# A second LayerNorm whose mean is taken out ahead: centred rows of w_down and a centred residual in a decoder layer on one Trainium2 core

## The chip, the cores and the metric

The kernel runs on one core of one Trainium2 chip. The metric is the device time of an execution in microseconds (us). Three executions of the kernel before took 368.48, 368.86 and 370.68 us; the median is 368.86. Profiles are of one execution each. Engines are named as in the profile: PE (TensorE), PEld (its weight loads), DVE (VectorE), ACT (ScalarE), POOL (GpSimd) and SP (SyncE, which issues the loads). L987 is line 987 of the kernel before.

## The reference

One layer over 256 positions of width 1024, all in float32: a mixer of attention and a short convolution, a LayerNorm, a gated feed-forward with a causal convolution of three taps, and a second LayerNorm. The part that matters here:

```python
x = layer_norm(DEEPNORM_ALPHA * x + mix, ln1_g[l], ln1_b[l])
u = causal_dwconv(x @ w_up[l], conv_w_ffn[l])
f = (jax.nn.silu(u[..., :D_FF]) * u[..., D_FF:]) @ w_down[l]
x = layer_norm(DEEPNORM_ALPHA * x + f, ln2_g[l], ln2_b[l])

def layer_norm(x, g, b):
    mu = jnp.mean(xf, axis=-1, keepdims=True)
    var = jnp.mean(jnp.square(xf - mu), axis=-1, keepdims=True)
    y = (xf - mu) * lax.rsqrt(var + LN_EPS) * g + b
```

`w_up` is 1024 by 5632, `w_down` 2816 by 1024. The mean over a row of `f` is `silu(..) * u` times the means over the rows of `w_down`; so if each row of `w_down` has its mean taken out, `f` has mean zero, and the same holds for `x` in the sum.

## The kernel before

Every product is made of three: each float32 operand is split into a high part (rounded by ACT) and a low part (the rest, made by DVE), and high by high, high by low and low by high are summed in PSUM. The weights come packed in chunks of 2048 columns (1 MB), each with two units of 1024; SP loads a chunk into one of three raw buffers (`issue_dma`, L175). `split_h` (L192) makes a unit's high part on ACT, `split_l` (L197) its low part on DVE; nine buffers each hold them until PE has used them. The next load into a raw buffer waits for the splits of both units that lay there.

The order of the feed-forward part is written out by hand. `seq` lists the units as PE uses them: for each pair i of w_up tiles a "g" and a "v" unit, and from i = 3 to 16 a unit d = i - 3 of w_down ("d"); the last eight units of w_down (TAIL) follow as "t". After PE's work of entry k, `slot(k, stages)` puts on ACT the first halves of the stages that are due, then splits so many units that they are four or five entries ahead of PE, and then the stages' DVE halves:

```python
for st, i in stages:
    FFN[st][0](i)
la = LA if k < 20 else LA + 1
while done["h"] < min(len(seq), k + la + 2):
    split_h(seq[done["h"]][2])
```

The four stages of a pair are: copy and sum of its PSUM banks (L807 on ACT, L811 on DVE), three taps of the convolution (L817; L823 and L825), SiLU and product (L830; L834), and the split of the result into an f tile (L837; L841). ACT and DVE run all this in the order in which it is issued. A pair's PSUM banks are two deep.

At the end, `finish(0)` runs the last eight units of w_down for the first 128 rows, one `slot` after each, and `finish(1)` for the other 128 rows: the left 512 columns first, then two pieces of 256 columns in banks of their own (`e`), so that DVE can work on one piece while PE makes the next. `residual` (L742, L744) adds `ALPHA * x1` to a bank and takes the statistics of the piece; `norm_stats` (L720, L721) joins the statistics on DVE and takes the power -1/2 on POOL; `norm_first` (L732) subtracts the mean and multiplies by ln2's factors, `norm_second` (L729) multiplies by the power and adds ln2's offsets; each piece is then stored, the last two from the queues of SP and ACT.

Of the kernel before, what the change touches and what calls it, by code (L numbers as in the profile page):

```python
# [8 lines left out]
F32 = mybir.dt.float32  # L9
# [3 lines left out]
AF = mybir.ActivationFunctionType  # L13
ALU = mybir.AluOpType

P = 128
S = 256
D = 1024
# [6 lines left out]
NP = DFF // P  # L25
ALPHA = 2.0 ** 0.25
EPS = 1e-5
# [110 lines left out]
def layer_kernel(ctx: ExitStack, tc: tile.TileContext, x, wpack, cpack, ln1_g, ln1_b, ln2_g, ln2_b, out):  # L138
    nc = tc.nc
# [4 lines left out]
    tmp = ctx.enter_context(tc.tile_pool(name="tmp", bufs=1))  # L144
# [5 lines left out]
    def acc_bank(name):  # L150
        return psum.tile([P, 512], F32, tag="acc", name=name)

    def ps_bank(name):
        return ps_pool.tile([P, 512], F32, tag="ps", name=name)

    def scratch(shape, name, bufs=None, tag="scr"):
        return tmp.tile(shape, F32, tag=tag, name=name, bufs=bufs or 6)
# [5 lines left out]
    chunks, plan_units, U = plan()  # L163
    blocks = transfers(chunks, plan_units)
    units = [dict(chunk=c, off=off, shape=(k, n), h=None, l=None) for c, off, k, n, _ in plan_units]
    raws = []
    XR_CHUNK = 20

    def issue_dma(c):
        while len(raws) <= c and len(raws) < len(chunks):  # L170
            i = len(raws)
            t = wp.tile([P, CHUNK], F32, tag="raw", name=f"raw{i}", bufs=RAW_BUFS)
            raws.append(t)
            for a, b, off in blocks[i]:
                nc.sync.dma_start(t[:, a:b], wpack[off:off + P * (b - a)].rearrange("(p n) -> p n", p=P))  # L175
            if i == XR_CHUNK:
                nc.sync.dma_start(xr, x[0].rearrange("(t p) d -> p t d", p=P))

    def alloc(u, part, tag):
        k, n = units[u]["shape"]  # L180
        units[u][part] = wp.tile([P, k, n], F32R, tag=tag, name=f"{tag}{u}", bufs=HL_BUFS)
# [6 lines left out]
    def split_h(u):  # L188

        issue_dma(units[u]["chunk"] + RAW_BUFS - 1)  # L190
        alloc(u, "h", "wh")
        nc.scalar.activation(units[u]["h"], raw_of(u), AF.Copy)  # L192

    def split_l(u):

        alloc(u, "l", "wl")
        nc.vector.tensor_tensor(units[u]["l"], raw_of(u), units[u]["h"].bitcast(F32), op=ALU.subtract)  # L197

    def raw_of(u):
        un = units[u]  # L200
        k, n = un["shape"]
        return raws[un["chunk"]][:, un["off"]:un["off"] + k * n].rearrange("p (k n) -> p k n", k=k)
# [43 lines left out]
    neghalf = cst.tile([P, 1], F32, name="neghalf")  # L246
# [25 lines left out]
    cs = cst.tile([P, 2, 2, 8], F32, name="cs")  # L272
# [55 lines left out]
    def cols_wide(u, bank, b):  # L328


        un = units[u]
        for k in range(un["h"].shape[1]):
            nc.tensor.matmul(bank, un["h"][:, k, :], b[:, k].rearrange("p a s -> p (a s)"), start=k == 0, stop=False)  # L333

    def cols_narrow(u, bank, b):

        un = units[u]
        nk = un["l"].shape[1]
        for k in range(nk):
            nc.tensor.matmul(bank[:, 0:S], un["l"][:, k, :], b[:, k, 0], start=False, stop=k == nk - 1)  # L340
# [138 lines left out]
    def slot(u, products=None):  # L479


        if products:
            products()
        mine = beside.pop(u, {})
        for f, a in mine.get("pe", []) + mine.get("act", []):
            f(*a)
        while done["h"] <= u + LA + 1:
            if units[done["h"]]["h"] is None:
                split_h(done["h"])
            done["h"] += 1  # L490
        while done["l"] <= u + LA:
            if units[done["l"]]["l"] is None:
                split_l(done["l"])
            done["l"] += 1
        for f, a in mine.get("dve", []):
            f(*a)
# [160 lines left out]
    for j in range(16):  # L657
        u = U[("g", 0)] + j
# [42 lines left out]
    for half in range(2):  # L701
        for e in range(2):
            ua, uc = U[("ao", half)] + e, U[("co", half)] + e
            for n in range(2):
# [4 lines left out]
                bank = ps_bank(f"y{i}")  # L709
# [7 lines left out]
    def norm_stats(r, stats, pieces):  # L717

        mv = tmp.tile([P, 4], F32, tag="mv", name="mv", bufs=4)
        nc.vector.bn_aggr(mv[:, 0:2], stats[:, 0:pieces, :])  # L720
        nc.gpsimd.tensor_tensor(mv[:, 3:4], mv[:, 1:2], neghalf, op=ALU.pow)  # L721
        return mv

    def norm_apply(o, r, mv, g, b):
        nc.vector.scalar_tensor_tensor(o, r, mv[:, 0:1], g, op0=ALU.subtract, op1=ALU.mult)
        nc.vector.scalar_tensor_tensor(o, o, mv[:, 3:4], b, op0=ALU.mult, op1=ALU.add)

    def norm_second(r, mv, ln, cs):
        nc.vector.scalar_tensor_tensor(r[:, cs], r[:, cs], mv[:, 3:4], ln[:, 1, cs], op0=ALU.mult, op1=ALU.add)  # L729

    def norm_first(r, mv, ln, cs):
        nc.vector.scalar_tensor_tensor(r[:, cs], r[:, cs], mv[:, 0:1], ln[:, 0, cs], op0=ALU.subtract, op1=ALU.mult)  # L732

    x1 = big.tile([P, 2, D], F32, tag="rows", name="x1")
    x1T = big.tile([P, KT, 2, S], F32R, tag="xT", name="x1T")

    def with_eps(stats):

        nc.vector.tensor_scalar(stats[:, 0, 2:3], stats[:, 0, 2:3], EPS * D, None, op0=ALU.add)

    def residual(t, nh, bank, res, r, stats, piece, c0, c1):
        nc.vector.scalar_tensor_tensor(r[:, c0:c1], res[:, t, c0:c1], ALPHA, bank[:, c0 - nh * 512:c1 - nh * 512],  # L742
                                       op0=ALU.mult, op1=ALU.add)
        nc.vector.bn_stats(stats[:, piece, :], r[:, c0:c1])  # L744
        if piece == 0:
            with_eps(stats)
# [44 lines left out]
    ln2 = big.tile([P, 2, D], F32, tag="e8", name="ln2")  # L791
# [87 lines left out]
    def ps_pair(name):  # L879
        return pairs.tile([P, 2, 512], F32, tag="pair", name=name)  # L880
# [7 lines left out]
    dacc = [[acc_bank(f"d{t}{nh}") for nh in range(2)] for t in range(2)]  # L888
# [19 lines left out]
    def take(n):  # L908
# [4 lines left out]
                pending.remove((stage, i))  # L913
        return out


    seq = []
    for c in range(1, NP // 2):
        for e in range(2):
# [3 lines left out]
            d = i - 3  # L923
# [21 lines left out]
    for k, (kind, i, u) in enumerate(seq[:tail_from]):  # L945
        if kind == "g":
            pair, first_unit = ps_pair(f"pb{i}"), u
            cols_wide(u, pair[:, 0], x1T)
        elif kind == "v":
            cols_wide(u, pair[:, 1], x1T)  # L950
            cols_narrow(first_unit, pair[:, 0], x1T)
            cols_narrow(u, pair[:, 1], x1T)
            PB[i] = pair
        else:
            down(i)
        if k == 0:
            up0_T(0)
            up0_T(1)
            pending.extend([(st, p) for p in range(2) for st in (1, 2, 3)])
        stages = take(2 if k > 11 or len(pending) > 6 else 1)  # L960
        if kind == "v":
            stages.insert(0, (0, i))
            pending.extend([(st, i) for st in (1, 2, 3)])
        slot(k, stages)


    def finish(t):
        r = x1[:, t]
        stats = tmp.tile([P, 4, 6], F32, tag="stats", name=f"rstats{t}", bufs=2)
        if t == 0:  # L970
            for k in range(TAIL):
                down(NP - TAIL + k, (t,))
                slot(tail_from + k, take(2))
            assert not pending
            for nh in range(2):
                residual(t, nh, dacc[t][nh], x1, r, stats, nh, nh * 512, nh * 512 + 512)
        else:
            for i in range(NP - TAIL, NP):
                down(i, (t,), (0,))
            nc.vector.scalar_tensor_tensor(r[:, 512:1024], x1[:, t, 512:1024], ALPHA, dacc[t][1], op0=ALU.mult, op1=ALU.add)  # L980
            for c in range(2):
                residual(t, 0, dacc[t][0], x1, r, stats, c, c * 256, c * 256 + 256)
            for c in range(2, 4):
                bank = ps_pair(f"e{c}")[:, 0]
                for i in range(NP - TAIL, NP):
                    down_part(i, bank, c)
                nc.vector.tensor_tensor(r[:, c * 256:c * 256 + 256], r[:, c * 256:c * 256 + 256], bank[:, 0:256], op=ALU.add)  # L987
                nc.vector.bn_stats(stats[:, c, :], r[:, c * 256:c * 256 + 256])
        mv = norm_stats(r, stats, 2 if t == 0 else 4)
        if t == 0:  # L990
            for c in range(2):
                cc = slice(c * 512, (c + 1) * 512)
                norm_apply(r[:, cc], r[:, cc], mv, ln2[:, 0, cc], ln2[:, 1, cc])
                nc.sync.dma_start(out[0, t * P:(t + 1) * P, cc], r[:, cc])
            return
        for c in range(2):
            norm_first(r, mv, ln2, slice(c * 512, c * 512 + 512))
        for cc, queue in ((slice(0, 640), nc.sync), (slice(640, D), nc.scalar)):
            norm_second(r, mv, ln2, cc)
            queue.dma_start(out[0, t * P:(t + 1) * P, cc], r[:, cc])  # L1000

    for t in range(2):
        finish(t)
# [42 lines left out]
```

## Time and profile before

| | |
|---|---|
| median of three runs | 368.86 us (368.48 to 370.68) |
| profiled execution | 369.0 us, span 367.1 us |
| granted TensorE clock, mean | 0.997 |
| PE busy | 358.0 us, 98% of the span |
| DVE busy | 294.9 us, 80% |
| ACT busy | 217.0 us, 59% |
| POOL busy | 7.0 us, 2% |
| read from HBM | 68.24 MB |

Times in the profile count from the first instruction; the span ends with the last. A row of the timeline has the start and the duration in us, the engine, the line, the operation, the tiles written and read, and the shapes; in square brackets stands how long the engine was idle ahead of it and what ended that. A row of a group has the count after x, then the busy time in us and the mean of one in ns. The next instruction of ACT or DVE can start before the last one's end, by about 0.1 us. A row of stretches has for each engine the busy time and the count of instructions, then the granted clock, the share of the DMA engines and GB/s.

### The profile page before, as it was taken

What the parts mean: (1) busy time and instruction counts of PE and PEld (TensorE: products, weight loads), DVE (VectorE), ACT (ScalarE), POOL (GpSimd) and SP (SyncE); (2) the same over time, 40 slices, a digit from 0 to 9 for tenths busy, and PEclk for the clock granted to TensorE, in tenths of its full rate; (3) what the DMA queues carried; (4) which work ended last, traced back from release to release, by engine and by line L of the source; (5) the groups of instructions that cost most, each with busy time, mean ns of one, the idle gap of its engine ahead of it and who ended that gap; (6) DMA issues with size and microseconds to landing.
All of it is one profiled execution on the core that took longest, in us unless ns stands there. A gap on an engine that the chain in (4) does not pass through costs nothing.

```text
span 367.1 us, 5335 instructions
## 1 busy us (share of the span) xinstructions
PE 358.0 (98%) x2022; PEld 312.2 (85%) x2022; DVE 294.9 (80%) x510; ACT 217.0 (59%) x372; POOL 7.0 (2%) x26
## 2 busy tenths in 40 slices
PE   8999999999999999999999999999999999999991
PEld 7888888888888899988888888888888888888891
DVE  4696887788895679869769988987869696999784
ACT  4685776747867654634266666575657566676300
POOL 2000000000000000102000000000000000000000
PEclk9999999999999999999999999999999999999998
DMA  7978565333853634596360835448182645662011
GB/s 263 356 292 318 180 225 211 114 114 129 331 214 130 221 124 137 190 357 224 124 223 12 341 121 221 153 193 309 46 334 90 254 140 204 228 237 108 0 59 57
DMA packets 11241, 69.63 MB, mean 190 GB/s; under 512 B 1232, under 2 KB 1616, under 8 KB 4176
## 3 DMA queue, kind: packets, MB, share of 16 engines
q1 hardware_dynamic: 10496, 67.00, 50.0%
q0 software_dynamic: 576, 2.10, 1.8%
q8 instruction: 16, 0.26, 0.3%
q10 hardware_dynamic: 144, 0.20, 0.1%
q14 instruction: 9, 0.07, 0.1%
HBM read 68.24 MB, written 1.05 MB: 189 GB/s over the span
## 4 chain that ended last, share of the span: by engine, by line
PE 97%; DVE 1%; DMA 1%; DVEq 0%; SPq 0%; issue 0%
PE pb L333 20%; PE pb L340 10%; PE g L333 8%; PE d L305 5%; PE d L306 5%; PE d L307 5%; PE g L340 4%; PE q L555 3%; PE k L555 3%; PE v L555 3%; PE b L333 2%; PE y L326 2%; PE y L325 2%; PE y L324 2%; PE c L333 2%; PE o L307 2%
## 5 line engine op out<-in xcount | busy, mean ns | idle before, releaser
L197 DVE TENSOR_TENSOR wl<-raw,wh 128x1024 fp32r<-128x1024 f32 x90 | 109.8, 1221 | 23.3 <-ACT wh L192 22.7
L192 ACT ACTIVATE wh<-raw 128x1024 fp32r<-128x1024 f32 x90 | 94.5, 1055 | 22.7 <-DMA raw<-in_wpack 22.6
L333 PE MATMUL pb<-x1T,wh 128*128 128x512 f32 x320 | 76.2, 390 | 0.0
L333 PEld LDWEIGHTS pb<-x1T,wh 128*128 128x128 f32 x320 | 59.7, 188 | 12.1
L220 DVE TENSOR_TENSOR wl<-raw,wh 128x1024 fp32r<-128x1024 f32 (+1 forms) x38 | 38.0, 1037 | 7.4 <-ACT wh L219 7.1
L340 PEld LDWEIGHTS pb<-x1T,wl 128*128 128x128 f32 x320 | 41.0, 191 | 1.6
L340 PE MATMUL pb<-x1T,wl 128*128 128x256 f32 x320 | 41.5, 283 | 0.0
L219 ACT ACTIVATE wh<-raw 128x1024 fp32r<-128x1024 f32 (+1 forms) x38 | 32.9, 904 | 14.3 <-DMA raw<-in_wpack 8.5
L333 PE MATMUL g<-xT,wh 128*128 128x512 f32 x128 | 31.4, 393 | 0.0
L305 PE MATMUL d<-wh,f 128*128 128x512 f32 x80 | 31.3, 391 | 0.0
L306 PE MATMUL d<-wl,f 128*128 128x512 f32 x80 | 31.3, 391 | 0.0
L307 PE MATMUL d<-wh,f 128*128 128x512 f32 x80 | 31.1, 389 | 0.0
L333 PEld LDWEIGHTS g<-xT,wh 128*128 128x128 f32 x128 | 23.3, 188 | 4.5
L807 ACT ACTIVATE fb<-pb 128x512 f32<-128x512 f32 x20 | 11.9, 595 | 23.8 <-PE pb L340 23.8
L825 DVE SCALAR_TENSOR_TENSOR fc<-fb,consts,fc 128x254 f32<-128x254 f32 x40 | 19.3, 484 | 1.4
L823 DVE SCALAR_TENSOR_TENSOR fc<-fb,consts,fc 128x255 f32<-128x255 f32 x40 | 19.1, 478 | 0.0
L817 ACT ACTIVATE fc<-fb,consts 128x256 f32<-128x256 f32 x40 | 17.9, 496 | 0.4 <-DVE fb L811 0.4
L307 PEld LDWEIGHTS d<-wh,f 128*128 128x128 f32 x80 | 15.0, 188 | 3.2
L305 PEld LDWEIGHTS d<-wh,f 128*128 128x128 f32 x80 | 15.1, 189 | 2.7
L306 PEld LDWEIGHTS d<-wl,f 128*128 128x128 f32 x80 | 15.1, 189 | 2.6
L340 PEld LDWEIGHTS g<-xT,wl 128*128 128x128 f32 x128 | 16.4, 191 | 0.6
L340 PE MATMUL g<-xT,wl 128*128 128x256 f32 x128 | 16.6, 283 | 0.0
(183 smaller groups left out, 606.1 us busy)
## 6 DMA issues: line engine op xcount, KB each, us to landing
raw<-in_wpack SPq DMA_DIRECT2D x55, 1024.0 KB, 4.9
raw<-in_wpack SPq DMA_DIRECT2D x6, 896.0 KB, 5.5
xr<-in_x SPq DMA_DIRECT2D x1, 1024.0 KB, 7.6
ln<-in_ln_g POOLq DMA_DIRECT2D x2, 512.0 KB, 5.6
ln<-in_ln_b POOLq DMA_DIRECT2D x2, 512.0 KB, 6.2
raw<-in_wpack SPq DMA_DIRECT2D x3, 256.0 KB, 3.4
raw<-in_wpack SPq DMA_DIRECT2D x1, 512.0 KB, 5.8
out<-x SPq DMA_DIRECT2D x2, 256.0 KB, 2.1
```

Source lines behind the costliest of these rows:

```text
L192: nc.scalar.activation(units[u]["h"], raw_of(u), AF.Copy)
L197: nc.vector.tensor_tensor(units[u]["l"], raw_of(u), units[u]["h"].bitcast(F32), op=ALU.subtract)
L219: nc.scalar.activation(h, src, AF.Copy)
L220: (eng or nc.vector).tensor_tensor(l, src, h.bitcast(F32), op=ALU.subtract)
L305: nc.tensor.matmul(o, ah, bh, start=start, stop=False)
L306: nc.tensor.matmul(o, ah, bl, start=False, stop=False)
L307: nc.tensor.matmul(o, al, bh, start=False, stop=stop)
L333: nc.tensor.matmul(bank, un["h"][:, k, :], b[:, k].rearrange("p a s -> p (a s)"), start=k == 0, stop=False)
L340: nc.tensor.matmul(bank[:, 0:S], un["l"][:, k, :], b[:, k, 0], start=False, stop=k == nk - 1)
L555: nc.tensor.matmul(banks[m][t], (xl if p == 2 else xh)[:, k, t * P:(t + 1) * P], wl if p == 1 else wh, start=k == 0 and p == 0, stop=k == ...
L823: nc.vector.scalar_tensor_tensor(c[:, 1:S], pb[:, a * S:a * S + S - 1], w_ffn(1, j), c[:, 1:S], op0=ALU.mult, op1=ALU.add)
L825: nc.vector.scalar_tensor_tensor(c[:, 2:S], pb[:, a * S:a * S + S - 2], w_ffn(0, j), c[:, 2:S], op0=ALU.mult, op1=ALU.add)
```

## The change

The units of w_down (`CENTRED`) are split so that each row has its mean taken out: ACT makes a first pass that writes the unit times -1/1024 and sums it (the sum is minus the mean, `m`), and a second pass that adds `m` as a bias and rounds; DVE's low part becomes (raw + m) - high. For each half of 128 rows, `centred(t)` makes `x1 = ALPHA * x1` in place on ACT with its sum, and minus the mean of it in a tile of one column; these are put on ACT's queue behind entries 14 and 17 of `seq`. In `finish` the residual is added with that mean (`add_residual`), the sum of squares over 1024, starting at LN_EPS, runs from piece to piece in `var` (`squares`), ln2's factors are multiplied piece by piece as soon as the squares of a piece are taken (`times_factors`), and POOL takes the power -1/2 of the last sum. `store` is the former `norm_second` with the store. PE's instructions and the loads are the same as before, in the same order.

```diff
+    CENTRED = {U[("dn", d)] + e for d in range(NP // 2) for e in range(2)}
...
         alloc(u, "h", "wh")
-        nc.scalar.activation(units[u]["h"], raw_of(u), AF.Copy)
+        h, raw = units[u]["h"], raw_of(u)
+        if u in CENTRED:
+            m = units[u]["m"] = tmp.tile([P, 1], F32, tag="wm", name=f"wm{u}", bufs=8)
+            nc.scalar.activation(h, raw, AF.Copy, scale=-1.0 / D, accum_out=m)
+            nc.scalar.activation(h, raw, AF.Identity, bias=m)
+        else:
+            nc.scalar.activation(h, raw, AF.Copy)
...
-        nc.vector.tensor_tensor(units[u]["l"], raw_of(u), units[u]["h"].bitcast(F32), op=ALU.subtract)
+        if u in CENTRED:
+            nc.vector.scalar_tensor_tensor(units[u]["l"], raw_of(u), units[u]["m"], units[u]["h"].bitcast(F32),
+                                           op0=ALU.add, op1=ALU.subtract)
...
+    def centred(t):
+        m = tmp.tile([P, 2], F32, tag="xm", name=f"xm{t}", bufs=2)
+        nc.scalar.activation(x1[:, t], x1[:, t], AF.Copy, scale=ALPHA, accum_out=m[:, 0:1])
+        nc.scalar.activation(m[:, 1:2], m[:, 0:1], AF.Copy, scale=-1.0 / D)
+        XM[t] = m[:, 1:2]
...
         slot(k, stages)
+        if k in (14, 17):
+            centred((k - 14) // 3)
...
+    def add_residual(t, cc, bank):
+        nc.vector.scalar_tensor_tensor(x1[:, t, cc], bank, XM[t], x1[:, t, cc], op0=ALU.add, op1=ALU.add)
+
+    def squares(t, cc, var, c):
+        r = x1[:, t, cc]
+        n = cc.stop - cc.start
+        nc.vector.tensor_tensor_reduce(out=scratch([P, n], f"sq{t}{c}"), in0=r, in1=r, scale=1.0 / D,
+                                       scalar=var[:, c - 1:c] if c else EPS, op0=ALU.mult, op1=ALU.add,
+                                       accum_out=var[:, c:c + 1])
+
+    def times_factors(t, cc):
+        nc.vector.tensor_tensor(x1[:, t, cc], x1[:, t, cc], ln2[:, 0, cc], op=ALU.mult)
+
+    def store(t, cc, rstd, queue):
+        r = x1[:, t, cc]
+        nc.vector.scalar_tensor_tensor(r, r, rstd, ln2[:, 1, cc], op0=ALU.mult, op1=ALU.add)
+        queue.dma_start(out[0, t * P:(t + 1) * P, cc], r)
...
-            for nh in range(2):
-                residual(t, nh, dacc[t][nh], x1, r, stats, nh, nh * 512, nh * 512 + 512)
+            for c, cc in enumerate(halves):
+                add_residual(t, cc, dacc[t][c])
+                squares(t, cc, var, c)
+                times_factors(t, cc)
...
-                nc.vector.tensor_tensor(r[:, c * 256:c * 256 + 256], r[:, c * 256:c * 256 + 256], bank[:, 0:256], op=ALU.add)
-                nc.vector.bn_stats(stats[:, c, :], r[:, c * 256:c * 256 + 256])
-        mv = norm_stats(r, stats, 2 if t == 0 else 4)
+                cc = slice(c * 256, c * 256 + 256)
+                nc.vector.tensor_tensor(x1[:, t, cc], x1[:, t, cc], bank[:, 0:256], op=ALU.add)
+                squares(t, cc, var, c - 1)
+                if c == 2:
+                    times_factors(t, cc)
+        last = 1 if t == 0 else 2
+        nc.gpsimd.tensor_tensor(var[:, 3:4], var[:, last:last + 1], neghalf, op=ALU.pow)
...
-        for c in range(2):
-            norm_first(r, mv, ln2, slice(c * 512, c * 512 + 512))
-        for cc, queue in ((slice(0, 640), nc.sync), (slice(640, D), nc.scalar)):
-            norm_second(r, mv, ln2, cc)
-            queue.dma_start(out[0, t * P:(t + 1) * P, cc], r[:, cc])
+            times_factors(t, slice(768, D))
+            store(t, slice(0, 640), rstd, nc.sync)
+            store(t, slice(640, D), rstd, nc.scalar)
```

More of the change, by code (lines that the diff above doesn't have):

```diff
@@ L191, in split_h @@
         alloc(u, "h", "wh")
-        nc.scalar.activation(units[u]["h"], raw_of(u), AF.Copy)
+        h, raw = units[u]["h"], raw_of(u)
[5 more added lines that the diff above has]
+            nc.scalar.activation(h, raw, AF.Copy)
     def split_l(u):
         alloc(u, "l", "wl")
-        nc.vector.tensor_tensor(units[u]["l"], raw_of(u), units[u]["h"].bitcast(F32), op=ALU.subtract)
+        if u in CENTRED:
+            nc.vector.scalar_tensor_tensor(units[u]["l"], raw_of(u), units[u]["m"], units[u]["h"].bitcast(F32),
+                                           op0=ALU.add, op1=ALU.subtract)
+        else:
+            nc.vector.tensor_tensor(units[u]["l"], raw_of(u), units[u]["h"].bitcast(F32), op=ALU.subtract)
     def raw_of(u):
@@ L726, in norm_apply @@
         nc.vector.scalar_tensor_tensor(o, o, mv[:, 3:4], b, op0=ALU.mult, op1=ALU.add)
[L728 to L732, printed above, removed]
     x1 = big.tile([P, 2, D], F32, tag="rows", name="x1")
@@ L914, in take @@
         return out
+    XM = {}
+    def centred(t):
[3 more added lines that the diff above has]
+        XM[t] = m[:, 1:2]
     seq = []
@@ L964, in layer_kernel @@
         slot(k, stages)
+        if k in (14, 17):
[14 more added lines that the diff above has]
+        queue.dma_start(out[0, t * P:(t + 1) * P, cc], r)
     def finish(t):
-        r = x1[:, t]
-        stats = tmp.tile([P, 4, 6], F32, tag="stats", name=f"rstats{t}", bufs=2)
+        var = tmp.tile([P, 4], F32, tag="var", name=f"var{t}", bufs=2)
+        halves = (slice(0, 512), slice(512, 1024))
         if t == 0:
@@ L979, in finish @@
                 down(i, (t,), (0,))
-            nc.vector.scalar_tensor_tensor(r[:, 512:1024], x1[:, t, 512:1024], ALPHA, dacc[t][1], op0=ALU.mult, op1=ALU.add)
-            for c in range(2):
-                residual(t, 0, dacc[t][0], x1, r, stats, c, c * 256, c * 256 + 256)
+            add_residual(t, halves[1], dacc[t][1])
+            add_residual(t, halves[0], dacc[t][0])
+            squares(t, halves[0], var, 0)
+            times_factors(t, halves[0])
             for c in range(2, 4):
@@ L986, in finish @@
                     down_part(i, bank, c)
-                nc.vector.tensor_tensor(r[:, c * 256:c * 256 + 256], r[:, c * 256:c * 256 + 256], bank[:, 0:256], op=ALU.add)
-                nc.vector.bn_stats(stats[:, c, :], r[:, c * 256:c * 256 + 256])
-        mv = norm_stats(r, stats, 2 if t == 0 else 4)
-        if t == 0:
[L991 to L996, printed above, removed]
-            norm_first(r, mv, ln2, slice(c * 512, c * 512 + 512))
-        for cc, queue in ((slice(0, 640), nc.sync), (slice(640, D), nc.scalar)):
-            norm_second(r, mv, ln2, cc)
-            queue.dma_start(out[0, t * P:(t + 1) * P, cc], r[:, cc])
+                cc = slice(c * 256, c * 256 + 256)
[5 more added lines that the diff above has]
+        nc.gpsimd.tensor_tensor(var[:, 3:4], var[:, last:last + 1], neghalf, op=ALU.pow)
+        rstd = var[:, 3:4]
+        if t == 0:
+            for cc in halves:
+                store(t, cc, rstd, nc.sync)
+        else:
+            times_factors(t, slice(768, D))
+            store(t, slice(0, 640), rstd, nc.sync)
+            store(t, slice(640, D), rstd, nc.scalar)
     for t in range(2):
```

## The prediction

> **What bounds the kernel now.** I read the share of busy time first, then the chain that ended last, then the stretch in which the changed weights are split, then the waits of ACT in that stretch.
>
> ```profile
> PE 358.0 (98%) x2022; PEld 312.2 (85%) x2022; DVE 294.9 (80%) x510; ACT 217.0 (59%) x372; POOL 7.0 (2%) x26
> ...
> PE 97%; DVE 1%; DMA 1%; DVEq 0%; SPq 0%; issue 0%
> ```
>
> ```profile
> 315.00:348.00 33.00, 33.00 (x177) 28.56 (x176) 29.53 (x49) 21.33 (x37) 0.00 (x0) 1.00 0.36 132
> ```
>
> ```profile
> ACT fb L807 <- PE pb L340: 23.8, 16, 2.8
> ACT wh L192 <- DMA raw<-in_wpack: 22.6, 16, 2.9
> ```
>
> PE is busy 98% of the span and 97% of the chain is PE. So there are two ways to change the time: make the 7.7 us after the last matmul shorter (367.1 less 359.4), or make PE wait where it does not wait now. From 315 to 348 us PE is busy for all of 33.00, but DVE is busy 29.53 and ACT 21.33: little is free beside PE. The last view is of 186 to 348 us, the feed-forward part: ACT waits there 23.8 us for PE and 22.6 us for loads of raw weights. That is ACT's reserve; the question is whether it lies where the change needs it.
>
> **The end: what is saved.** These rows are the timeline of the end.
>
> ```profile
> 359.11 0.28 PE L307 MATMUL e<-wh,f 128*128 128x256 f32 x1
> 359.42 0.42 DVE L987 TENSOR_TENSOR x<-x,e 128x256 f32<-128x256 f32 x1 [2.00 <-PE e L307]
> 359.88 0.43 DVE L988 BATCH_NORM_STATS2 rstats<-x 128x6 f32<-128x256 f32 x1
> 360.34 0.26 DVE L720 BATCH_NORM_AGGREGATE mv<-rstats 128x2 f32<-128x24 f32 x1
> 360.64 1.44 DVE L732 SCALAR_TENSOR_TENSOR x<-x,mv,ln 128x512 f32<-128x512 f32 x2
> 360.68 0.55 POOL L721 TENSOR_TENSOR mv<-mv,neghalf 128x1 f32<-128x1 f32 x1 [9.32 <-DVE mv L720]
> 362.18 1.41 DVE L729 SCALAR_TENSOR_TENSOR x<-x,mv,ln 128x640 f32<-128x640 f32 x2
> ```
>
> Today the last add is followed by statistics, aggregation, two multiplications by the factors (1.44) and the two last passes (L729), whose results go out. POOL's power lies under the 1.44. After the change the mean is already zero, so the last add is followed by the sum of squares, the power on POOL beside one multiplication of 256 columns, and the same two last passes. Sums of squares are the same instruction as the softmax's masked maximum, and an add of 256 columns has the price of the multiplication:
>
> ```profile
> L413 DVE CUSTOM_DVE_ANT_0 sm<-s,mask 128x256 f32<-128x256 f32 x8 | 3.0, 418 | 0.0
> L413 DVE DVE_READ_ACCUMULATOR2_ANT st<- 128x1 f32 x16 | 1.3, 82 | 0.0
> ```
>
> ```profile
> 177.13 0.57 POOL L721 TENSOR_TENSOR mv<-mv,neghalf 128x1 f32<-128x1 f32 x1 [8.94 <-DVE mv L720]
> ```
>
> ```profile
> 177.97 0.75 DVE L726 SCALAR_TENSOR_TENSOR x<-x,mv,ln 128x512 f32<-128x512 f32 x1
> ```
>
> Counted from the same start: squares at 359.88, their 0.418 and 0.082 end them at about 360.30 (the read overlaps a little). POOL started 0.08 after its releaser (360.60 to 360.68), so 360.38, and ends at 360.93. The multiplication, 360.30 to 360.72, is hidden under it. From POOL's end to the waiting DVE pass it was 0.27 in the first norm (177.70 to 177.97), where DVE itself was busy until 0.11 before; so 0.1 to 0.27. The last passes then start at 361.03 to 361.20 in place of 362.18: **a gain of 1.1 us**, bounds 0.8 (if the squares of two SBUF tiles take some 0.2 longer) and 1.15. The first half's norm costs about the same number of DVE passes as now and lies under PE's last 11 us.
>
> **The price: ACT goes twice over every w_down unit.** Each of the 22 units of w_down is now split by a first ACT pass that sums the row, a read of the accumulator, a wait of ACT for its own result, and a second pass with the mean as a pointer bias.
>
> ```profile
> 245.30 1.99 ACT L192 ACTIVATE wh<-raw 128x1024 fp32r<-128x1024 f32 x2
> ```
>
> ```profile
> L837 ACT ACTIVATE f<-ff 128x256 fp32r<-128x256 f32 x22 | 9.1, 412 | 2.2 <-DVE ff L834 2.2
> ...
> L424 ACT ACTIVATE sm<-sm,st 128x256 f32<-128x256 f32 x8 | 3.9, 495 | 0.0
> ...
> L424 ACT ACTIVATION_READ_ACCUMULATOR sm<-sm,st 128x1 f32 x16 | 3.0, 188 | 0.0
> ```
>
> Two passes of 1024 columns one behind the other take 1.99, so 0.95 each plus an end of 0.1. The accumulator read takes 0.19. An instruction with a pointer bias and accumulator (L424) is 0.08 longer than one without (L837) at the same 256 columns. The trace shows no wait of ACT for itself; between 0 and 0.2; I take 0.05, near the 0.04 that DVE pays behind its own result (359.84 to 359.88 above). One unit is then 0.95 + 0.19 + 0.05 + 1.04 = 2.23 in place of 0.95: **1.28 more**, bounds 1.0 and 1.5.
>
> On DVE the low half becomes one with a pointer scalar:
>
> ```profile
> L811 DVE TENSOR_TENSOR fb<-pb,fb 128x512 f32<-128x512 f32 x20 | 13.7, 686 | 3.4 <-ACT fb L807 2.9
> ...
> L726 DVE SCALAR_TENSOR_TENSOR x<-x,mv,ln 128x512 f32<-128x512 f32 x6 | 4.5, 752 | 0.8 <-POOL mv L721 0.5
> ```
>
> 0.752 against 0.686 at 512 columns is 0.07 more for an instruction, so 1.29 in place of 1.22, 1.5 us over 22 units.
>
> [...]
>
> **The last eight units.** Here the extra meets ACT's fixed order: per pair of w_up units the copy L807, the SiLU L830, a split, L837, two L817, a split. Before, the units 15 to 20 are split two to a pair while PE computes pairs 19 to 21.
>
> ```profile
> 326.19 0.60 ACT L807 ACTIVATE fb<-pb 128x512 f32<-128x512 f32 x1 [1.66 <-PE pb L340]
> ...
> 331.76 0.60 ACT L807 ACTIVATE fb<-pb 128x512 f32<-128x512 f32 x1 [1.59 <-PE pb L340]
> ...
> 337.33 0.60 ACT L807 ACTIVATE fb<-pb 128x512 f32<-128x512 f32 x1 [1.59 <-PE pb L340]
> ...
> 341.77 0.42 ACT L830 ACTIVATE fs<-fc 128x256 f32<-128x256 f32 x1 [0.47 <-DVE fc L825]
> 342.10 1.04 ACT L192 ACTIVATE wh<-raw 128x1024 fp32r<-128x1024 f32 x1
> ```
>
> ```profile
> 343.98 1.22 DVE L197 TENSOR_TENSOR wl<-raw,wh 128x1024 fp32r<-128x1024 f32 x1
> ```
>
> ```profile
> 346.67 0.39 PE L305 MATMUL d<-wh,f 128*128 128x512 f32 x1
> 346.90 0.39 PE L306 MATMUL d<-wl,f 128*128 128x512 f32 x1
> ```
>
> A pair is 5.57 us (331.76 to 337.33), and ACT waits 1.59 of it. Two units now cost it 2.56 more, so it falls behind by 0.97 per pair. Unit 14 fits into the 1.66 ahead of 326.19. After units 15 and 16 ACT is 0.97 late, after 17 and 18 it is 1.94, after 19 and 20 it is 4.50, less the 0.47 it waited ahead of 341.77: 4.03 late at the first pass of unit 21, and 5.31 at the end of its second: 343.14 becomes 348.45. DVE had started its low half 0.84 after that end, behind its own queue; now it starts at once, 348.50, and ends at 349.79. PE wants that half at 346.90. **Stall: 2.9 us.** Queued behind the late passes are L830, L837 and L817, so the last f tiles are late too, by the same amount and not in addition. With an extra of E for each of the seven units 15 to 21 this is 7 E less 6.1 (twice 1.59, 0.47, 0.84, and the 1.70 that the half was early, 345.20 to 346.90, less 0.1 for the longer half and a wait): nothing below 0.87, 0.9 at E = 1.0, 4.4 at E = 1.5.
>
> **What ACT carries into the last eight.** Units 0 to 13 come one to a group of 8.3 us, and two passes over x1 (some 1.4 each with read and sign) are put behind units 14 and 17 of the sequence. These rows are one lap of the three raw buffers, and the two waits after the middle units have ended:
>
> ```profile
> 287.30 1.06 ACT L192 ACTIVATE wh<-raw 128x1024 fp32r<-128x1024 f32 x1 [2.74 <-DMA raw<-in_wpack]
> ...
> 289.79 1.06 ACT L192 ACTIVATE wh<-raw 128x1024 fp32r<-128x1024 f32 x1 [1.12 <-DMA raw<-in_wpack]
> ...
> 292.26 1.06 ACT L192 ACTIVATE wh<-raw 128x1024 fp32r<-128x1024 f32 x1 [0.62 <-DMA raw<-in_wpack]
> ...
> 298.49 0.60 ACT L807 ACTIVATE fb<-pb 128x512 f32<-128x512 f32 x1 [1.54 <-PE pb L340]
> ```
>
> ```profile
> 315.06 0.60 ACT L807 ACTIVATE fb<-pb 128x512 f32<-128x512 f32 x1 [1.51 <-PE pb L340]
> ...
> 320.63 0.60 ACT L807 ACTIVATE fb<-pb 128x512 f32<-128x512 f32 x1 [1.75 <-PE pb L340]
> ```
>
> A lap splits two w_down units. The first (287.30) hides its 1.28 in the waits 1.12 and 0.62. The second lies between the last landing and the split that frees the next raw buffer; a late split there makes the next three loads late as well, and only the 1.54 at 298.49 pays it back. So nothing is carried if each lap pays its own (lower end 0); a full lap's 2.56 and both x1 passes, 2.8, less one 1.54 are carried if the loads move with it (upper end about 4). From 315 on there is time to recover, 1.51 and 1.75. I take the middle, **2.0**; PE itself has five units of lead and does not wait in the laps.
>
> **The sum**, against the profiled execution (369.0, span 367.1, so 1.9 around it): 369.0 + 2.9 + 2.0 - 1.1 = **372.8**. The median shown, 368.86, is 0.14 under that execution; I leave that aside. 1%, 3.7 us, is about what a measurement of this kernel tells from no change: the runs before span 368.48 to 370.68.
>
> **The rivals.** *Only the last eight count:* the laps pay their own extra, 369.0 + 2.9 - 1.1 = 370.8. For it: 46 us of waits of ACT; against it: the loads depend on the split that becomes late. *The ring of raw buffers starves:* 4 us or more are carried and the self-wait is at its upper end, 369.0 + 2.9 + 4.0 - 1.1 = 374.8, up to 376.3 with 4.4 in place of 2.9. For it: 16 waits for loads already. *The second pass is hidden, not slower:* if one unit costs less than 0.87 more, no weight is late and only the end's gain is left, 369.0 - 1.1 = 367.9; it decides below 1.03, where the stall equals the gain. Against it: the shortest spacing of such passes is 0.95, and the accumulator read comes on top. [...]
>
> *PE's clock falls in its new gaps.* The end of the trace shows what idleness does to it:
>
> ```profile
> 361.00:363.00 2.00, 0.00 (x0) 0.00 (x0) 1.90 (x4) 0.00 (x0) 0.23 (x1) 1.00 0.00 0
> 363.00:365.00 2.00, 0.00 (x0) 0.00 (x0) 0.59 (x2) 0.00 (x0) 0.00 (x0) 0.92 0.53 204
> ```
>
> PE ends at 359.4, and the clock is 1.00 up to 363 and 0.92 after. The gaps to come are about 1 us each, between bursts of six matmuls. If they added up to a fall all the same, and it took the clock as long to come back as it took to fall (some 3.6 us, 359.4 to 363), that stretch would take as long again: 376.4. [...]
>
> **How the numbers follow.** The forecast has 0.45, with a range of its own of 371.5 to 374.2; only the last eight 0.25; the starved ring 0.17; the hidden pass 0.07; the clock 0.04; half rate 0.02. Slower by over 1% begins at 372.55: 0.28 of the forecast, the ring, the clock and half rate make 0.51. Within 1% lie the rest of the forecast, the last eight and the hidden pass, 0.48; faster by over 1% 0.01, as the end gives 1.1 at most. The range 369.8 to 376.0 leaves out the hidden pass, half rate and the top of the ring.
>
> **What would show it.** In the changed profile: an ACT pair of passes 2.2 us long from first start to second end less 0.1; L807 no longer waiting for PE after 326 us; PE idle for low halves and f tiles of units 18 to 21, 1 us and less at a time, 3 to 7 in all; from the last matmul to the end about 6.6 us in place of 7.7. It is wrong if PE has no gaps before the last matmul, if gaps come already before 315 us, or if the end does not get shorter.

## Result and the profile after

The changed kernel takes **373.87 us** (median of 6 runs, 372.58 to 379.0), against 368.83 for the kernel before: a ratio of **1.013, 95% interval 1.0111 to 1.0149**. The 379.0 is one execution in a slower state, over 1.5% above the fastest of its kernel; it is left out of the ratio, and so is one of 373.46 in an experiment below. The profiled execution took 373.37, its span is 371.6, its granted clock 0.997. The forecast was 372.8.

The lines of the new kernel are shifted: before's plain high part L192 is L200; the two passes of a centred unit are L197 (with the accumulator's read) and L198; the low half L197 is now L209 (plain) and L206 (centred); the bank copy L807 on ACT is L813; PE's w_down matmuls L305 to L307 are L317 to L319.

First the share of busy time and the chain that ended last, from the page of after.

```profile
PE 359.9 (97%) x2022; PEld 311.1 (84%) x2022; DVE 295.3 (79%) x510; ACT 245.3 (66%) x422; POOL 7.7 (2%) x26
...
PE 49%; DMA 15%; ACT 15%; DVE 14%; issue 5%; SPq 0%; POOL 0%; POOLq 0%; DVEq 0%; ACTq 0%
```

ACT has 28 us more work (217.0 to 245.3) and still only 66%. But of the chain, which was 97% PE, 44% is now loads, ACT and DVE. Where it leaves PE is seen in the waits of PE over the whole span of after (two from ahead of the feed-forward part are left out), and in the stretches of its feed-forward part (PE, PEld, DVE, ACT, POOL, then clock, DMA share, GB/s):

```profile
PE d L318 <- DVE wl L206: 2.7, 4, 0.8
...
PE d L317 <- ACT wh L198: 0.8, 2, 0.6
```

```profile
186.00:320.00 134.00, 134.00 (x722) 116.06 (x721) 108.95 (x167) 101.48 (x167) 0.00 (x0) 1.00 0.53 191
320.00:335.00 15.00, 15.00 (x84) 13.05 (x83) 13.32 (x22) 13.31 (x24) 0.00 (x0) 1.00 0.52 193
335.00:364.74 29.74, 26.20 (x137) 20.74 (x135) 24.42 (x43) 15.79 (x28) 1.06 (x1) 1.00 0.13 51
```

From 186 to 335 us the profile shows no idle time of PE; from there to its last matmul it is idle 3.54, and every named wait is for a half of a w_down weight: four times a low half, twice a high half. These are the first and the last rows of PE's timeline through the gaps, with one gap shown in full:

```profile
342.30 0.39 PE L317 MATMUL d<-wh,f 128*128 128x512 f32 x1
343.18 0.50 PE L318 MATMUL d<-wl,f 128*128 128x512 f32 x1 [0.49 <-DVE wl L206]
343.52 0.39 PE L319 MATMUL d<-wh,f 128*128 128x512 f32 x1
...
352.93 0.39 PE L318 MATMUL d<-wl,f 128*128 128x512 f32 x1
```

Between the two ends lie 22 steps from start to start, 10.63 us. At the 0.227 that a step takes without a gap (346.67 to 346.90 to 347.13 in before) they would take 5.0. So 5.6 us are lost here, on six gaps and a seventh late start without a named wait. The idle time is less than what is lost, for two reasons. The profile counts idle time from the end of the matmul before, which it models 0.39 to 0.51 after that one's start, where the next would have started after 0.23: 1.5 us in the seven late starts. And the matmul behind a late one starts 0.34 after it (343.18 to 343.52): 0.6 in all.

The gauge used below is PE's stretch from the first `pb` matmul of the feed-forward part to the end of the last matmul: 186.84 to 359.39 before, 186.37 to 364.74 after, **5.83 longer**. Nearly all of it is the 5.6 above; some 0.15 is lost at 200.5 us, where a matmul starts 0.04 behind the end of a centred unit's second pass (200.48).

The end of after, from the timeline, answers to the rows of before's end:

```profile
364.46 0.28 PE L319 MATMUL e<-wh,f 128*128 128x256 f32 x1
364.78 0.42 DVE L1027 TENSOR_TENSOR x<-x,e 128x256 f32<-128x256 f32 x1 [1.47 <-PE e L319]
365.24 0.48 DVE L991 CUSTOM_DVE_ANT_0 sq<-x,var 128x256 f32<-128x256 f32 x1
365.65 0.08 DVE L991 DVE_READ_ACCUMULATOR2_ANT var<- 128x1 f32 x1
365.77 0.42 DVE L996 TENSOR_TENSOR x<-x,ln 128x256 f32<-128x256 f32 x1
365.81 0.79 POOL L1032 TENSOR_TENSOR var<-var,neghalf 128x1 f32<-128x1 f32 x1 [8.11 <-DVE var L991]
366.63 1.41 DVE L1000 SCALAR_TENSOR_TENSOR x<-x,var,ln 128x640 f32<-128x640 f32 x2 [0.44 <-POOL var L1032]
```

From the squares to the last passes it is 1.39 (365.24 to 366.63), where statistics to last passes took 2.30 (359.88 to 362.18): 0.91 gained. From the last matmul to the end it is 6.85 in place of 7.76.

The account of the profiled executions: 369.0, plus 5.83 in the feed-forward part, less 0.91 at the end, less 0.47 ahead of 186.84 and 0.1 around the span, is 373.4. The 0.47 lies where no edit of the change lies. It varies between executions: in the runs below that have three raw buffers the gauge starts at 186.05 to 187.20, so it is not put down to the change.

### The profile page after: what moved, and what is told of

Same layout as the page of the kernel before. It is cut to its first block, busy times and chain, and to the rows that moved or that the text cites. A ratio compares the mean times of both kernels' runs of the same rounds, so it can differ in the third digit from the quotient of the medians.

```text
span 371.6 us, 5372 instructions
## 1 busy us (share of the span) xinstructions
PE 359.9 (97%) x2022; PEld 311.1 (84%) x2022; DVE 295.3 (79%) x510; ACT 245.3 (66%) x422; POOL 7.7 (2%) x26
## 4 chain that ended last, share of the span: by engine, by line
PE 49%; DMA 15%; ACT 15%; DVE 14%; issue 5%; SPq 0%; POOL 0%; POOLq 0%; DVEq 0%; ACTq 0%
DMA raw<-in_wpack 15%; PE g L345 8%; DVE wl L209 5%; ACT wh L198 5%; ACT wh L197 4%; PE g L352 4%; PE q L567 3%; PE k L567 3%; PE v L567 3%; DVE wl L206 2%; PE b L345 2%; PE y L338 2%; PE y L337 2%; PE y L336 2%; PE c L345 2%
## 5 line engine op out<-in xcount | busy, mean ns | idle before, releaser
L209 DVE TENSOR_TENSOR wl<-raw,wh 128x1024 fp32r<-128x1024 f32 x68 | 83.0, 1220 | 12.8 <-ACT wh L200 12.5
L200 ACT ACTIVATE wh<-raw 128x1024 fp32r<-128x1024 f32 x68 | 71.5, 1055 | 12.3 <-DMA raw<-in_wpack 12.2
L206 DVE SCALAR_TENSOR_TENSOR wl<-raw,wm,wh 128x1024 fp32r<-128x1024 f32 x22 | 28.3, 1284 | 19.1 <-ACT wh L198 18.9
L317 PE MATMUL d<-wh,f 128*128 128x512 f32 x80 | 31.8, 397 | 0.9 <-ACT wh L198 0.8
L319 PE MATMUL d<-wh,f 128*128 128x512 f32 x80 | 31.3, 391 | 0.0
L197 ACT ACTIVATE wh<-raw 128x1024 fp32r<-128x1024 f32 x22 | 23.1, 1051 | 8.7 <-DMA raw<-in_wpack 8.7
L198 ACT ACTIVATE wh<-raw,wm 128x1024 fp32r<-128x1024 f32 x22 | 25.4, 1153 | 0.7
L317 PEld LDWEIGHTS d<-wh,f 128*128 128x128 f32 x80 | 15.1, 188 | 5.0 <-ACT wh L198 2.0
L319 PEld LDWEIGHTS d<-wh,f 128*128 128x128 f32 x80 | 15.0, 188 | 3.3
```

The lines of the kernel that those rows point to most:

```text
L197: nc.scalar.activation(h, raw, AF.Copy, scale=-1.0 / D, accum_out=m)
L198: nc.scalar.activation(h, raw, AF.Identity, bias=m)
L200: nc.scalar.activation(h, raw, AF.Copy)
L206: nc.vector.scalar_tensor_tensor(units[u]["l"], raw_of(u), units[u]["m"], units[u]["h"].bitcast(F32), op0=ALU.add, op1=ALU.subtract)
L317: nc.tensor.matmul(o, ah, bh, start=start, stop=False)
L319: nc.tensor.matmul(o, al, bh, start=False, stop=stop)
```

## Experiments

All start from the changed kernel but for one control. `CENTRED` is its set of w_down units that are split with the mean taken out: 22 units, of which 14 (0 to 13) lie in the middle and eight (14 to 21) are the last. A unit that is not centred keeps its share of the mean, and the new end does not take it out. "Longer" in the table is the gauge above, against before, from the one profiled execution of each kernel; the medians of the kernel before, to which the ratios are taken, lie between 368.44 and 368.83.

| kernel | us, median | ratio to before (95%) | longer, us | last matmul to end |
|---|---|---|---|---|
| change | 373.87 | 1.013 (1.0111 to 1.0149) | 5.83 | 6.85 |
| last eight centred | 370.2 | 1.0046 (1.003 to 1.0062) | 2.56 | 6.84 |
| first 14 centred | 368.51 | 1.0002 (0.9981 to 1.0024) | 1.01 | |
| none centred | 367.72 | 0.9979 (0.9968 to 0.999) | 0.00 | 6.85 |
| last eight, first pass over 768 columns | 369.09 | 1.0007 (0.9995 to 1.002) | 1.09 | |
| all 22, first pass over 512 columns | 368.94 | 0.9997 (0.9973 to 1.0021) | 0.01 | |
| x1's passes late | 374.01 | 1.0145 (1.0117 to 1.0174) | 6.45 | |
| four raw buffers | 374.69 | 1.0168 (1.0151 to 1.0185) | 2.79 | |
| before with four raw buffers | 372.93 | 1.0117 (1.0102 to 1.0132) | -0.01 | |
| mean in the low half | 367.61 | 0.9973 (0.996 to 0.9986) | 0.00 | 6.84 |

### Which units cost: the last eight, the first 14, none

```diff
-    CENTRED = {U[("dn", d)] + e for d in range(NP // 2) for e in range(2)}
+    CENTRED = {U[("dn", d)] + e for d in range((NP - TAIL) // 2, NP // 2) for e in range(2)}
```

> Only the last eight units of w_down (14 to 21) are centred; units 0 to 13 are split in one pass, so their share of the mean is left in. The x1 passes and the new end stay. Theory A (ACT's second pass makes the last eight late by 7 E - 6.1 us, and the first fourteen add a carried delay on top): PE gaps of 2.7 to 2.9 us, all after 335 us, the end 0.9 shorter, so 370.8 to 371.0. Theory B (the first fourteen do it, by way of late loads into the raw buffers): gaps below 0.5, so about 368.2.

```diff
+    CENTRED = {U[("dn", d)] + e for d in range((NP - TAIL) // 2) for e in range(2)}
```

> Only units 0 to 13 of w_down are centred; the last eight are split in one pass, so their share of the mean is left in. Theory A: ACT carries 2 to 3 us into the last eight, the low half of unit 21 was 1.7 early, so gaps of 0 to 1 us: 368.0 to 369.0. Theory B: most of the loss stays, gaps of 4 or more: 372 or above.

```diff
+    CENTRED = set()
```

> No unit of w_down is centred (its mean is left in); the x1 passes and the new end stay. It measures the end alone. Theory A: no gaps of PE, from the last matmul to the end 6.9 in place of 7.7, so 368.0. If the two x1 passes on ACT have a part in the loss (rival), gaps appear and it is 368.5 or more.

With none centred the end alone is left: PE's stretch has its old length, and the time falls by 0.7 (367.72 against 368.44), near the 0.91 that the end gains in the trace. With the last eight alone PE's stretch is 2.56 longer, a little less than the 2.7 to 2.9 expected. With the first 14 alone it is 1.01 longer, and the end's gain pays that: no difference. The two parts do not add: 2.56 and 1.01 are 3.6, and together they cost 5.83. What is left, 3.27 beyond the last eight, is lateness that ACT brings along and that matters only where the last eight then use up every wait. Unit 14's low half shows it, in before and in after:

```profile
325.82 1.22 DVE L197 TENSOR_TENSOR wl<-raw,wh 128x1024 fp32r<-128x1024 f32 x1
```

```profile
329.13 1.29 DVE L206 SCALAR_TENSOR_TENSOR wl<-raw,wm,wh 128x1024 fp32r<-128x1024 f32 x1 [0.21 <-ACT wh L198]
```

It is 3.3 late. With the first 14 alone it is 2.85 late (328.67), and with the last eight alone it is on time (325.57).

How the last eight spend the reserve is in ACT's timeline: the bank copies, in the kernel with the last eight alone, and then in the change.

```profile
325.92 0.60 ACT L813 ACTIVATE fb<-pb 128x512 f32<-128x512 f32 x1 [0.38 <-PE pb L352]
...
332.28 0.58 ACT L813 ACTIVATE fb<-pb 128x512 f32<-128x512 f32 x1
...
338.62 0.58 ACT L813 ACTIVATE fb<-pb 128x512 f32<-128x512 f32 x1
```

```profile
335.34 0.58 ACT L813 ACTIVATE fb<-pb 128x512 f32<-128x512 f32 x1
341.69 0.58 ACT L813 ACTIVATE fb<-pb 128x512 f32<-128x512 f32 x1
345.80 1.04 ACT L197 ACTIVATE wh<-raw 128x1024 fp32r<-128x1024 f32 x1
346.75 0.19 ACT L197 ACTIVATION_READ_ACCUMULATOR wh<-raw 128x1 f32 x1
346.97 1.15 ACT L198 ACTIVATE wh<-raw,wm 128x1024 fp32r<-128x1024 f32 x1
348.02 0.40 ACT L836 ACTIVATE fs<-fc 128x256 f32<-128x256 f32 x1
```

A pair takes ACT 6.34 to 6.36 where PE takes 5.57, so ACT loses 0.8 a pair once its waits are gone. In the first kernel there is still 0.38 of wait ahead of 325.92 (1.66 before), in the change none. A unit takes 2.22 from its first pass to the next instruction (345.80 to 348.02).

### The price of a unit: 768 columns, 512 columns

The price E, by which a unit is longer than 0.95, is changed by letting the first pass sum only part of the row (the mean is then that of a part).

```diff
     CENTRED as for the last eight alone
-            nc.scalar.activation(h, raw, AF.Copy, scale=-1.0 / D, accum_out=m)
+            nc.scalar.activation(h[:, :, 0:768], raw[:, :, 0:768], AF.Copy, scale=-1.0 / 768, accum_out=m)
```

> As the run with only the last eight units centred, but the first pass goes over 768 columns (the mean is that of three quarters of a row, and units 0 to 13 keep theirs). E falls from the 1.27 measured there to about 1.06. Theory A (slope of 7 us of PE's wait for each us of E, no carried delay): PE's wait falls from 2.56 to about 1.1, so 368.6 to 369.3, about like the kernel before: the point at which the price equals the gain of the end. Rival (a late unit costs one wait whatever its size): stays near 370.2.

```diff
     all 22 units
+            nc.scalar.activation(h[:, :, 0:512], raw[:, :, 0:512], AF.Copy, scale=-2.0 / D, accum_out=m)
```

> As the changed kernel, but the first pass of a centred unit runs over the first 512 columns only (the mean is that of half a row, so the normalised rows keep a part of their mean). E falls by some 0.43 to about 0.87, with the read, ACT's wait for itself and the second pass all still there. Theory A (7 E - 6.1): nothing or a few tenths in the last eight, little carried: 368.0 to 368.6, as without any centring. Rival (the read and the wait, or the pointer bias, make the loss, not the length): most of the loss stays, 371 or more.

One unit of each in ACT's timeline, 768 columns and then 512, each with the instruction behind it:

```profile
342.31 0.83 ACT L197 ACTIVATE wh<-raw 128x768 fp32r<-128x768 f32 x1
343.05 0.18 ACT L197 ACTIVATION_READ_ACCUMULATOR wh<-raw 128x1 f32 x1
343.26 1.16 ACT L198 ACTIVATE wh<-raw,wm 128x1024 fp32r<-128x1024 f32 x1
344.32 0.40 ACT L836 ACTIVATE fs<-fc 128x256 f32<-128x256 f32 x1
```

```profile
340.61 0.62 ACT L197 ACTIVATE wh<-raw 128x512 fp32r<-128x512 f32 x1
341.13 0.19 ACT L197 ACTIVATION_READ_ACCUMULATOR wh<-raw 128x1 f32 x1
341.35 1.15 ACT L198 ACTIVATE wh<-raw,wm 128x1024 fp32r<-128x1024 f32 x1
342.41 0.40 ACT L836 ACTIVATE fs<-fc 128x256 f32<-128x256 f32 x1
```

The first is 2.01 long (E = 1.06), the second 1.80 (E = 0.85). At E = 1.27 the last eight cost 2.56, at 1.06 they cost 1.09: 1.47 for 0.21, which is 7.0 for each us of E, the seven units of the forecast's formula. At 1.09 the price and the end's gain of 0.9 all but cancel, and the interval of the ratio holds 1. With E = 0.85 in all 22 units PE's stretch is as long as before (0.01) and PE waits for no weight: it is below the 0.87 of the forecast, and below the 0.90 at which the two measured points reach nothing (1.06 less 1.09 / 7.0). Unit 14's low half is on time as well (325.20), though all of the first 14 are centred, so nothing is carried at this price. But that is the profiled execution, which took 367.4; the median is 368.94, above what was expected by 0.3, and nine of the ten runs lie between 367.39 and 370.3, the tenth at 373.46. Why the runs of this kernel spread more than most is open, and so it is not shown that PE waits for nothing in the slower ones.

### What ACT carries: x1's passes, or the ring of raw buffers

The forecast held the two passes over x1 and the loads to be what makes ACT late ahead of unit 14. First x1's passes go behind ACT's last split, in the last stage:

```diff
-        if k in (14, 17):
-            centred((k - 14) // 3)
...
+            centred(0)
+            centred(1)
```

> As the changed kernel, but ACT's two passes over x1 stand behind its last split, where ACT has nothing else to do, not behind entries 14 and 17. Theory A: 1 us less is carried into the last eight (of 2.8, the rest is paid back in waits), so 372.3 to 372.9. Rival (a lap pays for any extra by itself, and the carried delay comes from the centred units alone): as the changed kernel, 373.4 to 374.

This missed. The time is that of the change (374.01) and unit 14 starts no earlier: its first pass is at 326.78 in the change, at 327.52 here. The passes over x1 add nothing that is seen to what is carried; that half of the reason falls.

Then a fourth raw buffer, for which there is room if one of nine high and low buffers goes, and as a control the kernel before with the same buffers:

```diff
-    RAW_BUFS, HL_BUFS = 3, 9
+    RAW_BUFS, HL_BUFS = 4, 8
```

> As the changed kernel, with four raw buffers in place of three (and eight buffers of high and low parts in place of nine, for the room). Theory A says that the delay is carried because a late split makes the next loads late: with one more buffer the loads come early enough, nothing is carried, and what stays is the last eight alone, 2.6, so 370.2 to 370.8. Rival (ACT itself is too slow in the laps, whatever the loads): no change, 373 to 374.

> The kernel before with the same four raw buffers and eight of high and low parts: a control for the last one. PE waits for nothing there, so all theories expect no change, 368.3 to 368.9; if the buffers themselves cost or gain, the last one has to be read against this.

Both totals missed, for a reason that the control shows. These are the waits of PE, of the change with four raw buffers and of before with four:

```profile
PE x1t L792 <- DVE x L738: 1.6, 2, 0.8
PE up L319 <- DVE x1T L232: 1.6, 1, 1.6
PE d L318 <- DVE wl L206: 1.4, 2, 0.8
```

```profile
PE x1t L786 <- DVE x L726: 1.6, 2, 0.8
PE up L307 <- DVE x1T L220: 1.6, 1, 1.6
```

The same two waits, around 172 to 179 us where x1 is transposed, come into both kernels. The first matmul of the gauge starts at 190.45 and 190.74, 3.6 and 3.9 later than 186.84. The control changes both counts at once, so it doesn't tell whether the missing high and low buffer or the fourth raw one is the cause. Against the control the change costs 374.69 less 372.93 = 1.76, in place of 5.0.

What the kernel was built for is in the waits of ACT between 186 and 356 us, of the change and then of the change with four raw buffers:

```profile
ACT wh L200 <- DMA raw<-in_wpack: 12.2, 10, 2.3
ACT wh L197 <- DMA raw<-in_wpack: 8.7, 6, 2.0
...
ACT fb L813 <- PE pb L352: 0.2, 1, 0.2
```

```profile
ACT fb L813 <- PE pb L352: 21.8, 13, 2.8
ACT fs L836 <- DVE fc L831: 4.9, 9, 0.9
```

With three buffers ACT still waits 20.9 for loads and next to nothing (0.2) for PE: it runs late throughout. With four it waits for no load, and 21.8 for PE. Ahead of the bank copy behind unit 14 it then waits 0.39, as with the last eight alone (0.38), and the stretch is 2.79 longer, near their 2.56. The 3.6 us by which PE begins later here, a head start for ACT and the loads, do not explain it: between 269 and 302 us ACT waits 2.16 for PE ahead of every bank copy, five times with no change, and an ACT that waits for PE each time has used up such a start and carries no lateness. **The carried lateness is that of the ring of three raw buffers.** The chain of after shows its form:

```profile
301.56 1.15 DVE wl L209
302.73 7.45 DMA raw<-in_wpack
310.19 1.07 ACT wh L200
311.29 1.23 DVE wl L209
...
313.45 1.15 DVE wl L209
314.61 4.78 DMA raw<-in_wpack
319.41 1.07 ACT wh L200
```

A late low half frees its buffer late, the load that was waiting for it starts late, and the next split waits for that load. A load takes 4.78 to 7.45 here. Over the whole span the median load of 1 MB takes 5.0, and 4.9 in before, where ACT is busy 59% and not 66%.

### The mean without a second pass

The mean may go into the low half alone: one ACT pass makes the high part of the raw weight and its sum, a pass over one column makes the negative mean, and DVE's low half, which reads the mean anyway, is (raw + mean) less the high part. The product is the same.

```diff
-            nc.scalar.activation(h, raw, AF.Copy, scale=-1.0 / D, accum_out=m)
-            nc.scalar.activation(h, raw, AF.Identity, bias=m)
+            nc.scalar.activation(h, raw, AF.Copy, accum_out=m[:, 0:1])
+            nc.scalar.activation(m[:, 1:2], m[:, 0:1], AF.Copy, scale=-1.0 / D)
```

> All 22 units are centred, but ACT makes only one pass over a unit: the high half is the rounded raw weight, its sum comes with that pass, one ACT instruction of one column scales it, and DVE's low half takes the mean along. E is then about 0.19 + 0.05 + 0.2 = 0.45 in place of 1.28. Theory A: below 0.87 nothing is late, no gaps, 367.9 to 368.2, which beats both kernels by a little. Rival: it is not the length of the pass but the extra read and ACT's wait for itself that stop the queue, then gaps of 1 to 3 remain and it is 369 to 371.

```profile
339.92 1.05 ACT L197 ACTIVATE wh<-raw 128x1024 fp32r<-128x1024 f32 x1
340.87 0.18 ACT L197 ACTIVATION_READ_ACCUMULATOR wh<-raw 128x1 f32 x1
341.08 0.20 ACT L198 ACTIVATE wm<-wm 128x1 f32<-128x1 f32 x1
341.32 0.42 ACT L836 ACTIVATE fs<-fc 128x256 f32<-128x256 f32 x1
```

A unit is 1.40 long (339.92 to 341.32), so E is 0.45, PE waits for no weight in the feed-forward part, and the time is that of the kernel with none centred: 367.61, ratio 0.9973 (0.996 to 0.9986), less than both kernels. The end's gain is what the change has to give, and this version keeps it.

## Why the prediction was right, and where it was off

- **The sum.** 372.8 forecast, 373.37 in the profiled execution, 373.87 in the median. The sign and the mechanism held: next to nothing (0.15) is lost ahead of 335 us, PE then waits in six gaps for the halves of w_down's last four units, and L813 has stopped waiting for PE. No wait is for an f tile, which had been named beside the low halves, and L813 stopped waiting from the first laps on (0.2 in all from 186 us), not only after 326. That the sum is off by only 0.6 is in part luck: the last eight are 0.34 under their term and the carried lateness 1.27 over, the end gives 0.19 less, and the 0.47 ahead of the feed-forward part was in no term.
- **The unit's price** was 1.28; it is 1.27 (2.22 less 0.95). The parts held too: the read 0.19, the pass with a pointer bias 0.10 longer, ACT's wait for its own sum 0.03 where 0.05 was taken (346.94 to 346.97).
- **The low half** was 1.29. The group of after has it:

```profile
L206 DVE SCALAR_TENSOR_TENSOR wl<-raw,wm,wh 128x1024 fp32r<-128x1024 f32 x22 | 28.3, 1284 | 19.1 <-ACT wh L198 18.9
```

  1.284, against 1.22 before: on two fp32 tiles of SBUF the form takes 5% longer than the plain subtraction of the same shape. No run shows a low half that takes twice as long, so half rate, which was given 0.02, falls.
- **The last eight** were 2.9 and measure 2.56 alone. The term 7 E has its slope (7.0); the constant is a little larger than 6.1 (6.3), for a pair takes ACT 6.35 and not 5.57 + 0.97 = 6.54. Before's rows tell where the 0.2 lies: the 1.59 count from the end of a split of 1.04, where the next instruction can start 0.95 behind its start (0.1), L837 stood 0.06 behind that as well (332.56 to 333.57), and two units cost 2.54 and not 2.56.
- **What ACT carries** is the term that was mis-sized: 2.0, the middle of bounds 0 and 4, and it is 3.27 (5.83 less 2.56). Its make-up was half wrong. The loads that move with the split are right, shown by the fourth buffer; x1's passes, 2.8 of its upper end, are not seen in it at all. Why the ring settles at some 3 us rather than more, and at nothing with E = 0.85, was not worked out by any run here.
- **The end** was 1.1 and is 0.91, within its bounds (0.8 to 1.15). What was mis-sized is POOL's power: 0.55 by the row of before, 0.79 here. From the start of the squares to POOL's start it is 0.57 and not 0.50; the last pass starts 0.03 behind POOL, sooner than the 0.1 to 0.27 taken. Before had shown a dearer power, in its first norm:

```profile
166.06 1.06 POOL L721 TENSOR_TENSOR mv<-mv,neghalf 128x1 f32<-128x1 f32 x1 [11.72 <-DVE mv L720]
```

- **The rivals.** Only the last eight: 370.8 forecast for a case that did not come, and 370.2 measured when it was made. The hidden pass: 367.9 forecast, and 367.6 and 367.7 measured with E = 0.45 and with nothing centred. The starved ring, 374.8, was nearer in its mechanism than its chance of 0.17 said: the time lies between it and the forecast. The clock stayed 1.00 in all three stretches above, through all six gaps (0.85 idle at most), so that rival falls. The fall took longer than its 3.6 us: in before the clock is still 1.00 from 364.0 to 364.5 and 0.50 from 365.0 on, 5.1 to 5.6 after the end of the last matmul (359.39). Its 376.4 reckons with that half clock.

## What to carry to other kernels

Idle time of an engine is no reserve by its sum. ACT had 46 us of it; what counted was the 1.6 us of wait per pair of w_up units, in an order that is fixed, and a ring of three buffers that passes each late release on to the next load. Compare the extra work of a period with the wait in that period, find the unit price at which it is used up (here some 0.9 us for the last eight, where the change needs 1.27), and look first for a cheaper way of doing the same (0.45, with the mean in the low half).

## What the runs showed of the hardware

- POOL's power of one column is not one price: 1.06 and 0.57 in the two halves of before's first norm, 0.55 in each half of its second, and 1.06 (in the stretch from 335 us above) and 0.79 in the second norm of after. Kind and shape of the instruction are the same; what differs was not looked into.
- A matmul that comes late costs more than the idle time that the profile shows: 3.54 us idle, 5.6 us lost. Matmuls follow each other every 0.23 us but are shown as 0.39 long, so a gap counts as idle only in part; and behind a late matmul, shown as 0.50, the next starts 0.34 later and not 0.23.
- ACT waits only 0.03 us for its own accumulator, but the read itself takes 0.19, a fifth of the pass over 1024 columns.
